# A hybrid SSD and attention trunk: the second projection issued between the first heads, and the diagonal products of a head pair taken in turn

## The chip, the cores and the metric

The kernel runs on one core of one Trainium2 chip. The metric is device time in microseconds, the median of several executions. A core has five engines that run at the same time, each with its own queue: TensorE (PE in the profile, with PEld for the loading of its stationary operand), VectorE (DVE), ScalarE (ACT), GpSimd (POOL) and SyncE (SP), which here only issues DMA transfers. Matrix products land in PSUM, which has eight banks here used as four "pa", three "pm" and one "po".

## The reference, cut to what matters

One sequence of 512 tokens with 1024 channels goes through two layers. The first layer mixes an RG-LRU and a Mamba-2 SSD, the second is softmax attention with 16 heads; each is followed by a SwiGLU FFN with 2816 hidden channels. Everything is float32. The change touches two places.

In the SSD, with 16 heads of 64 channels and chunks of 128 tokens, the part within a chunk is

```
y_diag = jnp.einsum('bclsgr,bcsgrp->bclgrp', cb[..., None] * decay, xdt)
```

that is, for each head and each of the four chunks, a 128 by 128 matrix (scores times decay) times the 128 by 64 inputs of that head.

In the attention layer the normed input is multiplied by one matrix that gives q, k and v of all heads; q and k are normed per head and partly rotated, then come scores, softmax and the product with v:

```
qkv = (h @ w_qkv).reshape(b, l, 3, ATT_HEADS, ATT_HEAD_DIM)
q = partial_rope(rmsnorm(qkv[:, :, 0], q_norm), pos) * (ATT_HEAD_DIM ** -0.5)
k = partial_rope(rmsnorm(qkv[:, :, 1], k_norm), pos)
```

The three dilated windows are merged into one softmax whose mask holds the logarithm of how many windows hold a key.

## The kernel before, in words

**Products.** Every large product is made of three fp32r products (low times high, high times low, high times high; `mm3`, L103 to L108, and L726 to L728 for q, k and v). For this each operand is split in two: `split` (L82 to L84) copies with rounding on ACT and subtracts on VectorE, or on GpSimd for the weights of the attention layer (`on_pool`, L80). `weight(i)` (L89) loads weight tile i and two ahead over SP's queue, 512 KB each, and splits them; raw, high and low tiles have three buffers each.

**SSD.** Two heads form a pair. `ssd_pair(j)` (L519) loads the cumulated decays of both heads, makes the decay matrices (L527 to L533) and leaves `ssd_out(j)` (L537) to be issued behind the next projection. `ssd_out` has the diagonal products, eight matmuls into one bank: head e of the pair writes partitions 64e to 64e+63, chunk c writes columns 128c to 128c+127, and its stationary operand has the 64 columns of that head (L543). Each of these fp32 matmuls shows up in the profile as two instructions. Then come three products with the carried states (L547) and three VectorE operations (L548 to L550). Pairs 0 to 3 run beside the RG-LRU, whose end (`lru_end`, L552) is a long chain on ACT and VectorE; pairs 4 to 7 run beside the gate projections.

**Attention.** The 16 heads are worked on in two halves of eight. `qkv_part(half, w)` (L711) gives four steps for w = 0, 1, 2 (q, k, v). A step takes one weight tile and issues 24 matmuls of 512 columns; four token tiles accumulate in the four "pa" banks over the four steps. The fourth step calls `finish_qk` (L737) for each of four token tiles: two ACT operations, a reduction, a power on GpSimd (L747), the scaling L748, and six small VectorE operations for the rotation (L752 to L757). For v it calls `finish_v` (L780), which writes the tiles v0 to v3; these have one buffer, so those of the second half are written when the first half has read its own.

`attend(half, between)` (L869) goes through eight heads:

```
            for h in range(first, first + 8):
                if h % 2 == 0 and h < first + 6:
                    pair_T(h // 2 + 1)
                if h < first + 7:
                    scores(h + 1)
                values(h)
                for st in between.get(h, ()):
                    st()
```

`pair_T` (L760) transposes q and k of a pair and splits them; `scores` (L796) makes the scores of a head (L808, L809) and its softmax on VectorE (L814, L816), ACT (L815) and GpSimd (L817); `values` (L821) transposes the probabilities (L835), splits them, and multiplies with v (L842, L843). Behind the first half stands the whole projection of the second half, 12 steps; the second half has parts of the output projection between its heads.

**What sets the order.** The program is unrolled. The framework that builds it arranges the instructions of each engine by itself ahead of time: the order in which they are written is their rank, and where a piece of higher rank is reckoned to wait for something, a piece of lower rank that is ready is put in. Buffers and data are guarded by semaphores. So the written order is a wish, and the order on TensorE can be read from the trace only.

Of the kernel before, what the change touches and what calls it, by code (L numbers as in the profile page):

```python
# [19 lines left out]
NT = T // P  # L20
# [38 lines left out]
def trunk(ctx: ExitStack, tc: tile.TileContext, a):  # L59
# [29 lines left out]
    def weight(i):  # L89
        while emitted[0] <= min(i + AHEAD, len(specs) - 1):  # L90
            j = emitted[0]
            src, n = specs[j]
            raw = wp.tile([P, WMAX], F32, tag="raw", bufs=NRAW, name=f"wr{j}")
            hi = wp.tile([P, WMAX], F32R, tag="whi", bufs=NSPL, name=f"wh{j}")
            lo = wp.tile([P, WMAX], F32R, tag="wlo", bufs=NSPL, name=f"wl{j}")
            step = n if j else n // 4
            for c in range(0, n, step):
                nc.sync.dma_start(out=raw[:, c:c + step], in_=src[:, c:c + step])
                split(raw[:, c:c + step], hi[:, c:c + step], lo[:, c:c + step], G if src.tensor.name in on_pool else V)
            w_of[j] = (hi, lo)  # L100
            emitted[0] += 1
        return w_of.pop(i, None)
# [54 lines left out]
    def pc(name, i=0, n=1):  # L157
        o, _ = _PV[name]
        return pv[:, o + i:o + i + n]
# [88 lines left out]
    with ExitStack() as rctx:  # L248
# [288 lines left out]
        def ssd_out(j, E, MT):  # L537
            g, jj = j // 4, j % 4
            pd = pm.tile([P, T], F32, tag="pm", name="ps_yd")
            for e in range(2):  # L540
                for c in range(NT):
                    s = slice(c * P, (c + 1) * P)
                    mm(pd[64 * e:64 * e + 64, s], lhsT=xdt[j][:, c, 64 * e:64 * e + 64], rhs=MT[e][:, s], start=True, stop=True)  # L543
            po = pm.tile([P, T], F32, tag="pm", name="ps_yo")
            for c in range(1, NT):
                s = slice(c * P, (c + 1) * P)
                mm(po[:, s], lhsT=prev[g, c - 1][:, jj * P:(jj + 1) * P], rhs=CT[g][:, s], start=True, stop=True)  # L547
            V.tensor_tensor(out=E[:, P:], in0=E[:, P:], in1=po[:, P:], op=ALU.mult)  # L548
            V.scalar_tensor_tensor(out=xs[j], in0=xs[j], scalar=pc("ssd_d", j), in1=pd, op0=ALU.mult, op1=ALU.add)
            V.tensor_tensor(out=xs[j][:, P:], in0=xs[j][:, P:], in1=E[:, P:], op=ALU.add)  # L550
# [128 lines left out]
    with ExitStack() as actx:  # L679
# [31 lines left out]
        def qkv_part(half, w):  # L711

            pss = []

            def step(kp):
                if kp == 0:
                    for t in range(NT):
                        pss.append(pa.tile([P, T], F32, tag="pa", name="ps_qkv"))
                wh, wl = weight(i_qkv[half, w, kp])
                for t in range(NT):  # L720
                    ts_ = slice(t * P, (t + 1) * P)
                    for k2 in range(2):
                        k = 2 * kp + k2
                        xh, xl = norm.hl[k]
                        cols = slice(k2 * T, (k2 + 1) * T)
                        mm(pss[t], lhsT=xl[:, ts_], rhs=wh[:, cols], start=(k == 0), stop=False)  # L726
                        mm(pss[t], lhsT=xh[:, ts_], rhs=wl[:, cols], start=False, stop=False)  # L727
                        mm(pss[t], lhsT=xh[:, ts_], rhs=wh[:, cols], start=False, stop=(k == KD - 1))  # L728
                if kp == 3:
                    for t in range(NT):  # L730
                        (finish_v if w == 2 else finish_qk)(half, w, t, pss[t])

            return [lambda kp=kp: step(kp) for kp in range(4)]
# [26 lines left out]
        def pair_T(pair):  # L760
            half, p = pair // 4, pair % 4
            for w in range(2):
                ps = pm.tile([P, T], F32, tag="pm", name="ps_qT")
                for t in range(NT):
                    nc.tensor.transpose(ps[:, t * P:(t + 1) * P], qk[half, w, t].rearrange("p h e -> p (h e)")[:, p * P:(p + 1) * P], ident)
                g = gains[w]

                hs_ = [ap_.tile([P, T], F32R, tag=f"hi{w}{e}", bufs=2, name="qk_hi") for e in range(2)]
                klo = None if w == 0 else kz[pair % 2]
                for e in range(2):  # L770
                    own = slice(64 * e, 64 * e + 64)
                    other = slice(64 - 64 * e, 128 - 64 * e)
                    S.activation(hs_[e][own], ps[own], AF.Copy, scale=g[own])  # L773
                    lo = hs_[e][other] if w == 0 else klo[e][own]
                    V.scalar_tensor_tensor(out=lo, in0=ps[own], scalar=g[own], in1=hs_[e][own].bitcast(F32), op0=ALU.mult, op1=ALU.subtract)
                    if w == 1:
                        S.activation(hs_[e][other], ps[own], AF.Copy, scale=g[own])
                qkT[pair, w] = hs_ if w == 0 else (hs_, klo)
# [73 lines left out]
        def out_proj(half, mp, after=None):  # L852
            w = weight(i_ao[half, mp])
            for m2 in range(2):
                ps = pa.tile([P, T], F32, tag="pa", name="ps_ao")
                for k in range(4):
                    c = (m2 * 4 + k) * P
                    mm3(ps, w, oT[4 * half + k], (slice(None), slice(c, c + P)), (slice(None), slice(None)), k == 0, k == 3)
                m = 2 * mp + m2
                V.tensor_tensor(out=x[m], in0=ps, in1=x[m], op=ALU.add)  # L860
                if after is not None:
                    after(m)
# [6 lines left out]
        def attend(half, between):  # L869
            first = 8 * half  # L870
            pair_T(first // 2)
            scores(first)
# [6 lines that stand above are left out]
                for st in between.get(h, ()):  # L879
                    st()  # L880

        attend(0, {})
        for w in range(3):
            for st in qkv_part(1, w):
                st()
        attend(1, {9: [lambda: out_proj(0, 0)], 12: [lambda: out_proj(0, 1)], 15: [lambda: out_proj(0, 2), lambda: out_proj(0, 3)]})
        for mp in range(4):
            out_proj(1, mp, norm3.feed)
# [94 lines left out]
```

## Time and profile before

| | before |
|---|---|
| median of 3 runs | 1359.38 us (1357.98 to 1360.65) |
| profiled execution | 1356.76 us, its span 1355.0 us |
| TensorE busy | 1329.4 us (98%) |
| VectorE / ScalarE / GpSimd busy | 794.5 / 573.2 / 151.3 us |
| mean granted TensorE clock | 0.998 |

Times in the rows count from the first instruction. The duration of a matmul in the profile is its way through the engine, and matmuls overlap: a 512-column product of the fp32r kind has a duration of 0.39 us while the next one starts 0.23 us after it. An engine is shown as idle only where no instruction is on its way. L-numbers are lines of the listing above; names such as ps_yd, ps_qkv, ps_s, ps_pT and ps_o are the PSUM tiles of the diagonal products, the projection, the scores, the transposed probabilities and the outputs.

### The profile page before, as it was taken

Reading aid. Unit: us, or ns where it says so; the run is one execution under the profiler, and the core shown is the slowest. Engines: PE = TensorE matmul, PEld = TensorE weight load, DVE = VectorE, ACT = ScalarE, POOL = GpSimd, SP = SyncE. Lnnn points to the kernel's source line nnn. Section 1 sums busy time; section 2 is a strip of 40 time slices with the busy share of each in tenths; the row PEclk is TensorE's granted clock in tenths of the full one; section 3 lists DMA queues with packets and bytes.
Section 4 is the critical chain, followed back from the end, with each engine's and each line's share of the span. In section 5 each row is a group of like instructions: output and inputs, shape, how many; then the busy total and the mean of one; then the engine's idle time right before and its main releaser. Section 6 shows DMA issues by size and latency. Waiting matters only on the chain.

```text
span 1355.0 us, 15685 instructions
## 1 busy us (share of the span) xinstructions
PE 1329.4 (98%) x6058; PEld 1074.7 (79%) x6058; DVE 794.5 (59%) x1332; ACT 573.2 (42%) x842; POOL 151.3 (11%) x127
## 2 busy tenths in 40 slices
PE   8999989999999999999999999999999999999998
PEld 6877767888888888888888877777788888888886
DVE  7887799865444434434453778788764434444442
ACT  6743867433333222312233479658643212222221
POOL 0000000000000000000005755554200000000000
PEclk9999999999999999999999999999999999999999
DMA  6322222532233333332232221221133333333232
GB/s 238 110 92 80 94 78 77 172 94 94 93 94 93 94 93 100 92 105 93 88 100 94 80 76 48 63 78 47 32 109 93 93 95 99 97 86 107 93 100 72
DMA packets 38554, 126.50 MB, mean 93 GB/s; under 512 B 4288, under 2 KB 5056, under 8 KB 38352
## 3 DMA queue, kind: packets, MB, share of 16 engines
q1 hardware_dynamic: 38480, 125.51, 29.7%
q8 instruction: 47, 0.77, 0.2%
q14 instruction: 27, 0.22, 0.1%
HBM read 123.36 MB, written 2.13 MB: 93 GB/s over the span
## 4 chain that ended last, share of the span: by engine, by line
PE 83%; DVE 8%; ACT 6%; POOL 1%; issue 1%; DMA 0%; SPq 0%; POOLq 0%; DVEq 0%; ACTq 0%
PE ps_pr L106 24%; PE ps_pr L107 24%; PE ps_pr L108 24%; ACT s L815 1%; PE ps_qkv L726 1%; PE ps_qkv L728 1%; PE ps_qkv L727 1%; POOL qrs L747 1%; DVE q L748 1%; ACT qk_hi L773 1%; PE ps_pT L835 1%; PE ps_yd L543 1%; PE ps_o L842 1%; ACT ph L83 1%; DVE q L756 1%
## 5 line engine op out<-in xcount | busy, mean ns | idle before, releaser
L83 ACT CAST wh<-wr 128x1024 fp32r<-128x1024 f32 (+2 forms) x223 | 228.1, 1024 | 629.8 <-PE ps_pr L108 396.1
L106 PE MATMUL ps_pr<-xh,wl 128*128 128x512 f32 x1056 | 415.9, 394 | 11.9 <-DVE wl L84 11.2
L107 PE MATMUL ps_pr<-xl,wh 128*128 128x512 f32 x1056 | 414.3, 392 | 0.9 <-DVE xl L183 0.9
L108 PE MATMUL ps_pr<-xh,wh 128*128 128x512 f32 x1056 | 412.8, 391 | 0.0
L84 DVE TENSOR_TENSOR wl<-wr,wh 128x1024 fp32r<-128x1024 f32 (+2 forms) x191 | 225.9, 1183 | 52.1 <-ACT wh L83 51.6
L106 PEld LDWEIGHTS ps_pr<-xh,wl 128*128 128x128 f32 x1056 | 199.2, 189 | 55.1 <-DVE wl L84 12.1
L107 PEld LDWEIGHTS ps_pr<-xl,wh 128*128 128x128 f32 x1056 | 199.2, 189 | 43.9 <-DVE xl L183 2.3
L108 PEld LDWEIGHTS ps_pr<-xh,wh 128*128 128x128 f32 x1056 | 199.1, 189 | 42.0 <-issue 0.7
L108 PE MATMUL ps_pr<-ah,wh 128*128 128x512 f32 x352 | 138.7, 394 | 0.0
L106 PE MATMUL ps_pr<-ah,wl 128*128 128x512 f32 x352 | 138.7, 394 | 0.0
L107 PE MATMUL ps_pr<-al,wh 128*128 128x512 f32 x352 | 138.7, 394 | 0.0
L84 POOL TENSOR_TENSOR wl<-wr,wh 128x1024 fp32r<-128x1024 f32 x32 | 79.1, 2475 | 395.7 <-ACT wh L83 392.6
L669 DVE TENSOR_TENSOR x<-ps_pr,x 128x512 f32<-128x512 f32 x48 | 33.2, 692 | 127.6 <-PE ps_pr L108 127.6
L661 DVE TENSOR_TENSOR tu<-ps_pr,nrb 128x512 f32<-128x512 f32 x44 | 30.4, 692 | 130.7 <-PE ps_pr L108 130.7
L659 DVE TENSOR_TENSOR tg<-ps_pr,nrb 128x512 f32<-128x512 f32 x44 | 30.4, 692 | 93.9 <-PE ps_pr L108 93.9
L107 PEld LDWEIGHTS ps_pr<-al,wh 128*128 128x128 f32 x352 | 65.8, 187 | 16.3
L108 PEld LDWEIGHTS ps_pr<-ah,wh 128*128 128x128 f32 x352 | 65.8, 187 | 16.3
L106 PEld LDWEIGHTS ps_pr<-ah,wl 128*128 128x128 f32 x352 | 65.8, 187 | 16.2
L726 PE MATMUL ps_qkv<-wh,xl 128*128 128x512 f32 x192 | 75.6, 394 | 0.6 <-ACT q L740 0.6
L728 PE MATMUL ps_qkv<-wh,xh 128*128 128x512 f32 x192 | 75.5, 393 | 0.0
L727 PE MATMUL ps_qkv<-wl,xh 128*128 128x512 f32 x192 | 75.5, 393 | 0.0
L726 PEld LDWEIGHTS ps_qkv<-wh,xl 128*128 128x128 f32 x192 | 36.1, 188 | 7.9 <-ACT q L740 1.0
(232 smaller groups left out, 1580.5 us busy)
## 6 DMA issues: line engine op xcount, KB each, us to landing
wr<-in_w_gu SPq DMA_DIRECT2D x88, 512.0 KB, 3.5
wr<-in_w_in SPq DMA_DIRECT2D x35, 512.0 KB, 3.5
wr<-in_w_dn SPq DMA_DIRECT2D x32, 448.0 KB, 3.4
wr<-in_w_qkv SPq DMA_DIRECT2D x24, 512.0 KB, 3.5
wr<-in_w_out SPq DMA_DIRECT2D x16, 512.0 KB, 3.5
wr<-in_w_dn SPq DMA_DIRECT2D x16, 512.0 KB, 3.5
x<-in_xT SPq DMA_DIRECT2D x16, 256.0 KB, 3.2
bcs<-csd SPq DMA_DIRECT2D x16, 256.0 KB, 4.4
```

The lines of the kernel that those rows point to most:

```text
L83: S.copy(hi, src)
L84: eng.tensor_tensor(out=lo, in0=src, in1=hi.bitcast(F32), op=ALU.subtract)
L106: mm(ps, lhsT=wl[ws], rhs=xh[xs], start=start, stop=False)
L107: mm(ps, lhsT=wh[ws], rhs=xl[xs], start=False, stop=False)
L108: mm(ps, lhsT=wh[ws], rhs=xh[xs], start=False, stop=stop)
L543: mm(pd[64 * e:64 * e + 64, s], lhsT=xdt[j][:, c, 64 * e:64 * e + 64], rhs=MT[e][:, s], start=True, stop=True)
L659: V.tensor_tensor(out=tg, in0=pg, in1=rb, op=ALU.mult)
L661: V.tensor_tensor(out=tu, in0=pu, in1=rb, op=ALU.mult)
L669: V.tensor_tensor(out=x[m], in0=ps, in1=x[m], op=ALU.add)
L726: mm(pss[t], lhsT=xl[:, ts_], rhs=wh[:, cols], start=(k == 0), stop=False)
L727: mm(pss[t], lhsT=xh[:, ts_], rhs=wl[:, cols], start=False, stop=False)
L728: mm(pss[t], lhsT=xh[:, ts_], rhs=wh[:, cols], start=False, stop=(k == KD - 1))
```

## The change

In `ssd_out` the two loops change places, so that the diagonal products of the two heads follow each other chunk by chunk. In the attention layer the 12 steps of the second half's projection are put into `attend(0, ...)`: two steps behind head 0, one behind head 1, and so on (2, 1, 2, 1, 2, 1, 2, 0), eleven in all; the last step, which holds `finish_v`, stands behind the first half as before. No operation is added or removed.

```
-            for e in range(2):
-                for c in range(NT):
+            for c in range(NT):
+                for e in range(2):
...
-        attend(0, {})
-        for w in range(3):
-            for st in qkv_part(1, w):
-                st()
+        steps = [st for w in range(3) for st in qkv_part(1, w)]
+        at_head, k = {}, 0
+        for h, n in enumerate((2, 1, 2, 1, 2, 1, 2, 0)):
+            at_head[h] = steps[k:k + n]
+            k += n
+        attend(0, at_head)
+        for st in steps[k:]:
+            st()
```

## Rows read from the trace of the kernel before

**Rows 1.** The page's first lines and its chain of waits, by engine and by line.

```profile
span 1355.0 us, 15685 instructions
PE 1329.4 (98%) x6058; PEld 1074.7 (79%) x6058; DVE 794.5 (59%) x1332; ACT 573.2 (42%) x842; POOL 151.3 (11%) x127
...
PE 83%; DVE 8%; ACT 6%; POOL 1%; issue 1%; DMA 0%; SPq 0%; POOLq 0%; DVEq 0%; ACTq 0%
```

**Rows 2.** The chain that ended last, in order of time, from 130 to 300 us: start, duration, what, and the count of instructions merged.

```profile
137.35 1.51 PE ps_yd L543 x16
...
157.64 0.87 ACT wh L83
...
192.94 1.51 PE ps_yd L543 x16
...
204.83 0.69 ACT ti L483
...
248.64 1.02 PE ps_yd L543 x8
...
262.74 1.51 PE ps_yd L543 x16
...
289.46 1.51 PE ps_yd L543 x16
```

**Rows 3.** Instructions of the tile ps_yd in three stretches of the block that starts at 262.67 us: stretch, its length, then busy time and count of each engine (an instruction counts in each stretch that it touches).

```profile
262.67:263.16 0.49, 0.49 (x4) 0.49 (x5) 0.00 (x0) 1.00 0.16 67
263.16:263.60 0.44, 0.44 (x10) 0.44 (x9) 0.00 (x0) 1.00 0.83 344
263.60:264.18 0.58, 0.58 (x8) 0.41 (x4) 0.00 (x0) 1.00 1.02 417
```

**Rows 4.** TensorE in order of time: start, duration, line, operation, tiles, count, and in brackets the idle time before it with what ended it. First a pair that is absent from rows 2, then the longest wait of the recurrent layer.

```profile
159.25 1.58 PE L543 MATMUL ps_yd<-bcs,xdt 128*64 128x128 f32 x16
...
182.20 0.79 PE L106 MATMUL ps_pr<-xh,wl 128*128 128x512 f32 x1 [4.16 <-DVE wl L84]
```

**Rows 5.** Busy time of every engine in the first half's heads, in the stretch behind them, and in the second half's heads: stretch, length, then PE, PEld, DVE, ACT, POOL with counts, granted clock, DMA share, GB/s.

```profile
791.00:866.00 75.00, 70.81 (x384) 55.19 (x383) 62.70 (x186) 63.78 (x139) 38.73 (x42) 1.00 0.17 50
866.00:899.00 33.00, 33.00 (x147) 27.28 (x146) 21.36 (x39) 14.19 (x19) 21.40 (x10) 1.00 0.26 81
899.00:972.00 73.00, 69.70 (x378) 54.10 (x377) 57.64 (x160) 57.82 (x130) 28.78 (x37) 1.00 0.13 44
```

**Rows 6.** The same two first stretches for the instructions of the tile ps_qkv alone (PE, PEld, DVE, ACT).

```profile
791.00:866.00 75.00, 40.19 (x144) 25.07 (x143) 2.58 (x4) 3.46 (x5) 1.00 0.17 50
866.00:899.00 33.00, 33.00 (x147) 27.28 (x146) 0.36 (x1) 4.81 (x7) 1.00 0.26 81
```

**Rows 7.** TensorE's two largest waits from 791 to 899.5 us: who waited for whom, total us, times, longest us.

```profile
PE ps_pT L835 <- DVE m L814: 2.7, 3, 2.3
PE ps_s L808 <- DVE kz L775: 0.4, 1, 0.4
```

**Rows 8.** TensorE in order of time: the one place where a projection waits for its bank, then two short waits among the heads and the longest.

```profile
773.61 0.50 PE L726 MATMUL ps_qkv<-wh,xl 128*128 128x512 f32 x1 [0.55 <-ACT q L740]
...
811.95 0.63 PE L835 MATMUL ps_pT<-cst,s 128*128 128x128 f32 x4 [0.19 <-DVE m L814]
...
819.65 0.39 PE L728 MATMUL ps_qkv<-wh,xh 128*128 128x512 f32 x1
820.22 0.30 PE L808 MATMUL ps_s<-kz,qk_hi 128*128 128x128 f32 x1 [0.18 <-DVE qk_hi L775]
...
856.06 0.40 PE L728 MATMUL ps_qkv<-wh,xh 128*128 128x512 f32 x1
858.77 0.87 PE L835 MATMUL ps_pT<-cst,s 128*128 128x128 f32 x6 [2.31 <-DVE m L814]
```

**Rows 9.** GpSimd in order of time from 846 us on, then VectorE in the stretch of the longest wait.

```profile
846.69 2.39 POOL L84 TENSOR_TENSOR wl<-wr,wh 128x1024 fp32r<-128x1024 f32 x1 [0.88 <-ACT wh L83]
849.07 0.69 POOL L817 TENSOR_SCALAR s<-s,m 128x512 f32<-128x512 f32 x1
...
853.51 2.40 POOL L84 TENSOR_TENSOR wl<-wr,wh 128x1024 fp32r<-128x1024 f32 x1
...
853.78 2.21 DVE L756 TENSOR_TENSOR q<-rtmp 128x64 f32<-128x64 f32 x1
855.91 0.21 DVE L757 TENSOR_TENSOR q<-rtmp 128x64 f32<-128x64 f32 x1
```

**Rows 10.** VectorE in order of time behind the first half's heads: its instructions above 2 us. Then the page of line L748: shortest, median and longest duration in ns.

```profile
868.60 2.48 DVE L84 TENSOR_TENSOR xl<-o,xh 128x512 fp32r<-128x512 f32 x1 [1.46 <-ACT xh L83]
...
881.67 2.88 DVE L748 TENSOR_TENSOR q<-q,qrs 128x512 f32<-128x512 f32 x1 [1.53 <-POOL qrs L747]
...
890.22 2.87 DVE L748 TENSOR_TENSOR q<-q,qrs 128x512 f32<-128x512 f32 x1 [1.25 <-POOL qrs L747]
...
893.02 2.42 DVE L756 TENSOR_TENSOR q<-rtmp 128x64 f32<-128x64 f32 x1
895.50 2.42 DVE L752 TENSOR_TENSOR rtmp<-q,rope1c 128x64 f32<-128x64 f32 x1
...
L748 DVE TENSOR_TENSOR q<-q,qrs x16: 674/693/2877, 747.3 to 890.2; 128x512 f32<-128x512 f32 x16
```

**Rows 11.** The page's DMA issues of the projection's weights: count, KB each, us from issue to landing.

```profile
wr<-in_w_qkv SPq DMA_DIRECT2D x24, 512.0 KB, 3.5
```

## The prediction, as it was put on record

> **What bounds the kernel now.** The page's first lines and its chain come first: TensorE is busy for 1329.4 of 1355.0 us, and 83% of the chain is its own work [rows 1]. So a part of the change is worth what it takes off TensorE's queue, or off TensorE's waits, in a stretch where nothing else ends last; that has to be read stage by stage. No instruction is added or taken away, so only overlap and waits can change. For the SSD I read the chain in order of time [rows 2], since it tells which blocks of diagonal products lie on the path, and the instructions of ps_yd by stretches [rows 3]. For the attention layer I read the busy time of all engines in three stretches [rows 5]: in the heads of the first half TensorE is idle for 75.00 - 70.81 = 4.2 us with VectorE at 84% and ScalarE at 85%, and in the 33 us behind them it is never idle. Then its waits [rows 7, 8], and what the engines before it were doing [rows 9, 10].
>
> The rows on ps_qkv are the surprise: the projection of the second half, written behind the first half's heads, is not run there alone. Of its 288 matmuls some 138 (144 in the stretch, less 6 that end the first half's own v) lie among the heads, and the rest behind [rows 6]. The framework fills the waits with it already: 138 / 24 = 5.8 of 12 steps, where the new text asks for 11.
>
> **Part 1: the diagonal products in turn.** A block has 16 instructions, eight for each head of the pair. Where only one head's eight stand together they take 1.02 us on the chain (248.64); where all sixteen stand together they take 1.51 us, and not twice as much [rows 2]. The stretches tell why: for the first 0.49 us four instructions of ps_yd are touched, then ten in 0.44 us [rows 3], so the second head's instructions, which write the other 64 partitions, run beside the first head's last ones. Written in turn, both heads should run side by side from the start, and a block should take what one head takes: 1.51 - 1.02 = 0.49 us less. Bounds: 0 if the overlap needs the long run of one head; 0.49; below nothing, if taking turns kept the two heads apart altogether, a block would take two runs of eight, 2.04 us, 0.53 more than now, 2.7 us in the five blocks that count. I take 0.49, the nearest row: in the stretch of ten both heads are at work together.
>
> Which blocks count: the three from 262.74 to 289.46 lie on the chain with TensorE work on both sides, 3 x 0.49 = 1.47. Those at 137.35 and 192.94 lie on it too, ahead of the points where the chain goes over to ScalarE (157.64 and 204.83) [rows 2]: ScalarE starts earlier by as much, 0.98. The block at 159.25 comes after the chain has left TensorE, which then waits 4.16 us for the split of a weight tile that is late on VectorE [rows 4]; the 0.49 makes this wait longer and is worth nothing, and the same holds for the fourth pair, behind 204.83. The block at 248.64 stands there as eight because the second head's matrix was not reckoned to be ready; I count 0, as it will be late in any order. Sum: 2.45 us, between +2.7 and -3.4 (seven blocks).
>
> The Trainium skill speaks against this part: "TensorE: Matmul & The Clock Gate", section "Part 3: Packing small matmuls", says that matmuls start and end strictly in program order, and that a load of weights overlaps a running matmul only where the row group differs, which it does not here. By that rule the order of the two heads is worth 0, a rival below. The same section says that outputs on different partition groups of PSUM run at the same time, and by that the 2.45 stand. The trace agrees with the second: sixteen take 1.51 us and not 2 x 1.02.
>
> **Part 2: the moved projection.** TensorE's work is the same. What can go is the idle time among the heads, 4.2 us [rows 5]. Of it 2.31 is one wait at 858.77 and 0.45 the wait of the very first scores for kz (0.4 in rows 7), ahead of any moved step. The other 1.4 us is in twelve short pieces, like those at 811.95 and 820.22. Such a piece costs more than is shown: at 820.22 the next start comes 0.57 us after the last one, in place of 0.23, so 0.34 is lost where 0.18 is shown as idle [rows 8]. The 0.16 on top belongs to each. Two pieces (0.25) fall into heads 0 and 1, at 811.95 and before it, where the order can hardly change. The ten left are 1.2 + 10 x 0.16 = 2.8 us. A step now outranks the next heads, so TensorE has 24 matmuls of 0.23 us between a head's scores and its values, and softmax gets the time: I take all 2.8 off. Bounds: 0, and 5.8 (all idle but the first scores, 3.74, and 13 x 0.16).
>
> What the move adds. Besides the 24 matmuls, each step issues one 512 KB transfer, 3.5 us to landing [rows 11], one ScalarE cast and one GpSimd subtraction. On SP nothing else stands in these stretches but later weights in the same order, so the transfers cost nothing. On GpSimd a split takes 2.39 us and a head's normalisation stands behind it (846.69, 849.07) [rows 9]; today six splits lie among the heads, tomorrow about eleven. TensorE's next matmuls cover that, as they do in this case. The fourth step of a group brings four finishes with it. The q group's four lie among the heads already, the k group's four move there from the 33 us in which TensorE waits for nothing and VectorE is at 65% [rows 5]. The wait of 2.31 us shows the price: at 853.78 VectorE's L756 takes 2.21 us (its like, L757, takes 0.21 right behind) while GpSimd splits a weight tile (853.51 to 855.91); behind it in VectorE's queue stand the next tiles' steps and the reciprocals and maxima of softmax, for which ScalarE and then TensorE wait [rows 8, 9]. Behind the heads five such instructions stand [rows 10]. One of them per group is the nearest count (one stall of 2.31 + 0.16 = 2.5 us from the q group's finishes); half of it I take as covered by the steps that now rank ahead: +1.2. Bounds: 0 and 5 x 2.5 = 12.4.
>
> The last step brings finish_v behind the first half's last values, and the output projection needs its four banks. A projection that waited for a bank lost 0.55 us [rows 8]; I take that, +0.55. Bounds: 0, and the 2.31 of the longest wait.
>
> Sum of part 2: -2.8 + 1.2 + 0.55 = -1.05.
>
> **Sum.** -2.45 - 1.05 = -3.5 us. Against its own time, the profiled execution's 1356.76 (span 1355.0 and 1.76 around), that is 1353.3. That execution lies 2.6 below the median of the runs, so on the median of 1359.38 it is 1355.9. A measurement of this kernel tells some 0.2% (2.7 us) from no change: the forecast is on the edge of what can be seen.
>
> **Rivals.**
>
> Everything goes well (16%): all waits among the heads that can go do, 5.8, with no new stall, and seven blocks give 3.4: 9.2 less, 1350.2. For it: TensorE's work sets these stretches and ScalarE and VectorE have 16% to spare. Against: the order is fixed ahead and does not know of L756 at 2.21 us.
>
> Slower, by the k finishes (18%): four of the five long VectorE instructions of rows 10 now stop softmax in the midst of the heads and TensorE each time by 2.5 us, 9.9 in all; less 2.45, 2.8 and plus 0.55 that is +5.2, 1364.6. At two stalls it is a draw, from the third on it is slower. For it: 881.67, 890.22, 893.02 and 895.50 are all of the k group, L748 at 2.88 where its median is 0.69. Against: they stand close to each other behind a string of splits at full speed of the projection, and splits will come more slowly between heads. The Trainium skill, "SBUF — State Buffer", section "Who interferes with whom", has the rule behind it: a VectorE instruction with two SBUF inputs and a GpSimd instruction that reads SBUF exclude each other for their whole length. By it each of the moved finishes can meet a split, and the time would be that of this rival; the trace agrees at 853.78.
>
> The order of the heads is worth nothing on TensorE (15%): part 2 alone, 1358.3. For it: only long runs show the overlap. Against: 1.51 against 1.02 us.
>
> The move changes nothing (11%): the framework has filled the waits already, and goes on filling with what is ready; gain and loss of part 2 cancel, part 1 alone, 1356.9.
>
> **How the numbers follow.** The forecast has 40%, its own range 1353.9 to 1357.9 (one term of part 2 or two blocks more or less). Faster by over 0.2% (below 1356.7): three quarters of the forecast, 0.30, the first rival, 0.16, half of the last, 0.05, and 0.02 of the third: 0.53. Within 0.2%: 0.10 of the forecast, 0.12 of the third, 0.06 of the last, 0.01 of the second: 0.29. Slower: 0.17 of the second, 0.01 of the third: 0.18. The range of 8 in 10 leaves out half of the first rival and most of the second: 1351 to 1362.
>
> **What would show it.** In the profile after: the sixteen instructions of a block within 1.02 us, and five or more blocks that are shorter on the chain; the wait at 182.20 not shorter than 4.16 less 0.1. Among the first heads some 264 matmuls of ps_qkv and not 138, a stretch with less than 2.5 us of idle TensorE, and the pieces of 0.1 to 0.2 us fewer; the k group's L748 to L757 between softmax operations, with at most one above 2 us that TensorE waits behind. Wrong would be: blocks of 1.5 us; several waits of 2 us or more of ps_pT or ps_o; a wait of TensorE for finish_v; or the same 4 us of idle time at other places.

## The result and the profile after

The changed kernel takes 1372.24 us (median of 4 runs, 1371.53 to 1373.55) against 1359.43 us for the kernel before on the same chip: ratio 1.0096, 95% interval 1.0078 to 1.0113, so 13 us slower. The forecast was 1355.9 in a range of 1351 to 1362; the sign was wrong. The profiled execution took 1372.17 us. Its page, first lines and chain of waits, beside [rows 1]:

```profile
span 1370.1 us, 15687 instructions
...
PE 1331.2 (97%) x6058; PEld 1074.8 (78%) x6058; DVE 791.3 (58%) x1332; ACT 574.0 (42%) x842; POOL 150.3 (11%) x127
...
PE 83%; DVE 9%; ACT 5%; POOL 2%; issue 1%; DMA 0%; SPq 0%; POOLq 0%; DVEq 0%; ACTq 0%
```

The span grew by 15.1 us and TensorE's busy time by 1.8, so nearly all of it is idle time of TensorE, or 13.3 us. On the chain GpSimd goes from 1% to 2% and VectorE from 8% to 9%. First the SSD: the chain in order of time, as in [rows 2].

```profile
137.46 1.02 PE ps_yd L543 x16
...
193.10 1.02 PE ps_yd L543 x16
...
261.82 0.36 PE ps_yd L543 x2
262.19 0.42 PE ps_yo L547 x2
262.61 1.02 PE ps_yd L543 x14
...
275.29 1.02 PE ps_yd L543 x16
...
288.16 1.02 PE ps_yd L543 x16
```

Sixteen instructions now take 1.02 us where they took 1.51, as forecast, in four of the five blocks that were to count. The fifth (262.74 before) was taken apart by the framework: two of its instructions, then two of ps_yo, then the rest, 0.36 + 1.02 = 1.38 us for its own. The late weight split still ends the wait of 4.16 us in [rows 4]. TensorE goes on 0.37 us earlier than before, and the wait became longer by about what the block before it got shorter:

```profile
181.83 0.80 PE L106 MATMUL ps_pr<-xh,wl 128*128 128x512 f32 x1 [4.63 <-DVE wl L84]
```

The attention layer then starts 1.75 us earlier (first transpose of q at 789.68 and not 791.43), so everything that was lost was lost behind that. TensorE's waits from 789 to 1000 us, total, times and longest, against [rows 7], which end with the first half (of the 15.5 us, 14.6 fall there):

```profile
PE ps_pT L835 <- DVE m L814: 15.5, 7, 8.0
PE ps_s L808 <- DVE qk_hi L775: 1.8, 2, 1.7
```

Before, the transposes of the probabilities waited 2.7 us for softmax maxima in the first half's heads. Now two of these waits are 8.0 and 5.7 us long. The stretches around the first, with columns as in [rows 5], the one behind the second, and the second half's heads at the end:

```profile
829.00:837.80 8.80, 8.80 (x46) 7.51 (x44) 6.36 (x14) 4.57 (x8) 5.25 (x3) 1.00 0.16 49
837.80:846.20 8.40, 0.37 (x3) 0.04 (x1) 6.54 (x19) 1.41 (x3) 5.00 (x4) 0.73 0.24 73
846.20:851.90 5.70, 5.70 (x19) 4.74 (x20) 3.88 (x19) 3.73 (x10) 3.04 (x5) 0.50 0.00 1
...
882.14:886.00 3.86, 3.86 (x11) 3.20 (x12) 2.36 (x11) 1.35 (x3) 1.77 (x2) 0.50 0.08 33
...
915.00:988.00 73.00, 69.88 (x379) 54.14 (x378) 56.40 (x158) 57.82 (x130) 28.84 (x37) 1.00 0.12 37
```

For 8.4 us TensorE does next to nothing (0.37 us), ScalarE little (1.41), and even VectorE and GpSimd are not full (6.54 and 5.00 of 8.40): a chain that goes back and forth between engines. The second half's heads are as before (69.88 of 73.00 busy against 69.70). VectorE in order of time from 829 us on, with only the lines that carry the argument:

```profile
829.08 0.68 DVE L744 TENSOR_REDUCE qss<-qsq 128x8 f32<-128x512 f32 x1
...
831.73 0.69 DVE L748 TENSOR_TENSOR q<-q,qrs 128x512 f32<-128x512 f32 x1 [1.76 <-POOL qrs L747]
...
833.20 2.10 DVE L753 TENSOR_TENSOR rtmp<-q,rope0s 128x64 f32<-128x64 f32 x1
...
838.26 0.69 DVE L748 TENSOR_TENSOR q<-q,qrs 128x512 f32<-128x512 f32 x1 [0.71 <-POOL qrs L747]
...
840.87 2.82 DVE L748 TENSOR_TENSOR q<-q,qrs 128x512 f32<-128x512 f32 x1 [1.25 <-POOL qrs L747]
...
845.36 0.68 DVE L814 CUSTOM_DVE_ANT_0 s<-ps_s,cst 128x512 f32<-128x512 f32 x1
```

and GpSimd beside it:

```profile
830.05 1.65 POOL L747 TENSOR_TENSOR qrs<-qss,mhalf 128x8 f32<-128x8 f32 x1 [3.00 <-DVE qss L745]
832.82 2.39 POOL L84 TENSOR_TENSOR wl<-wr,wh 128x1024 fp32r<-128x1024 f32 x1 [1.13 <-ACT wh L83]
836.59 1.64 POOL L747 TENSOR_TENSOR qrs<-qss,mhalf 128x8 f32<-128x8 f32 x1 [1.37 <-DVE qss L745]
839.18 1.66 POOL L747 TENSOR_TENSOR qrs<-qss,mhalf 128x8 f32<-128x8 f32 x1 [0.95 <-DVE qss L745]
840.81 2.33 POOL L84 TENSOR_TENSOR wl<-wr,wh 128x1024 fp32r<-128x1024 f32 x1
```

This is the finish of the q group. The scores of the next head are ready at 837 us, but its first maximum (L814, 845.36) stands in VectorE's queue behind the q group's token tiles. From 829.08 to 845.36, 16.3 us, VectorE is on them (and on one short addition that ends a head), and only about half of that is work. It waits three times for the power on GpSimd, 1.76 + 0.71 + 1.25 = 3.7 us, and twice an instruction is held up while GpSimd splits a weight tile: L753 takes 2.10 us (its like take 0.22), L748 takes 2.82 (0.69), so 1.88 + 2.13 = 4.0 us. Without these 7.7 us the maximum could have come that much earlier, if nothing else had held the tiles, and that is most of TensorE's wait of 8.03 us. This is a reckoning; the runs below test it. TensorE in order of time:

```profile
837.77 0.40 PE L728 MATMUL ps_qkv<-wh,xh 128*128 128x512 f32 x1
846.19 1.09 PE L835 MATMUL ps_pT<-cst,s 128*128 128x128 f32 x4 [8.03 <-DVE m L814]
...
847.93 0.63 PE L728 MATMUL ps_qkv<-wh,xh 128*128 128x512 f32 x1
848.36 0.63 PE L726 MATMUL ps_qkv<-wh,xl 128*128 128x512 f32 x1
```

After the wait the next matmuls start 0.43 us apart and not 0.23: the granted clock of that stretch is 0.50, the 1.2 GHz level, and it had been 1.00, the 2.4 GHz level, until TensorE stopped. Seven matmuls of 512 columns took from 846.93 to 850.07, 3.1 us in place of 1.6, so the stall cost at least 1.5 us more than it shows, and the stretch at 0.50 lasts until 851.90.

The k group's finish does the same a second time: L748 waits 1.82 and 1.53 us, and lasts 2.82 in the second case, 2.13 too long; together 5.5 us, against 5.71 us of the wait that follows.

```profile
873.61 0.69 DVE L748 TENSOR_TENSOR q<-q,qrs 128x512 f32<-128x512 f32 x1 [1.82 <-POOL qrs L747]
...
877.36 2.82 DVE L748 TENSOR_TENSOR q<-q,qrs 128x512 f32<-128x512 f32 x1 [1.53 <-POOL qrs L747]
...
881.31 0.68 DVE L814 CUSTOM_DVE_ANT_0 s<-ps_s,cst 128x512 f32<-128x512 f32 x1
```

```profile
882.14 1.09 PE L835 MATMUL ps_pT<-cst,s 128*128 128x128 f32 x4 [5.71 <-DVE m L814]
```

The clock is at 0.50 behind this wait too, from 882.14 to 886.00. With that the loss adds up. From the first transpose of q of the first half to that of the second, before and after:

```profile
791.43:899.47 108.04, 103.85 (x530) 82.50 (x529) 84.10 (x226) 77.98 (x157) 60.13 (x52) 1.00 0.19 59
```

```profile
789.68:914.87 125.19, 107.77 (x530) 85.98 (x528) 81.09 (x227) 78.87 (x157) 59.06 (x52) 0.93 0.16 55
```

The stretch grew by 17.2 us for the same 530 instructions of TensorE: its idle time from 4.2 to 17.4 us, 13.2 more, and its busy time by 3.9 us, for which the 9.6 us at clock 0.50 have room (half of them, 4.8, at most).

Each engine's order is fixed when the program is built, so it can be read without a clock. VectorE's queue in the first half's heads, one letter per instruction: S a softmax maximum (L814), p the split of transposed probabilities, o the addition that ends a head, Q a scaling L748 (one per token tile's finish), V a v finish. Both strings begin with the first head's splits.

```
before  pppSoSSSpppoSSSSpppSoSSSpppSoSSSQpppQSoSSSpppSQSoSSpppQpoppoQQQQVVVV
after   pppoSSSSpppoSSSSpppQoQQSQSSSpppoSSSSpppoQQSQQSSSpppSoSSSpppopppVoVV
```

Before, the q group's four finishes stand singly among the later heads, and the k group's four behind all heads. After, three tiles of the q group (with one addition between) and two of the k group stand in one run ahead of the maxima of a head that is waited for, and the next tile's reduction with them.

### The profile page after: what moved, and what is told of

Read it like the earlier page. It is cut to its first block, busy times and chain, and to the rows that moved or that the text cites. A ratio compares the mean times of both kernels' runs of the same rounds, so it can differ in the third digit from the quotient of the medians.

```text
span 1370.1 us, 15687 instructions
## 1 busy us (share of the span) xinstructions
PE 1331.2 (97%) x6058; PEld 1074.8 (78%) x6058; DVE 791.3 (58%) x1332; ACT 574.0 (42%) x842; POOL 150.3 (11%) x127
## 3 DMA queue, kind: packets, MB, share of 16 engines
HBM read 123.36 MB, written 2.13 MB: 92 GB/s over the span
## 4 chain that ended last, share of the span: by engine, by line
PE 83%; DVE 9%; ACT 5%; POOL 2%; issue 1%; DMA 0%; SPq 0%; POOLq 0%; DVEq 0%; ACTq 0%
PE ps_pr L106 24%; PE ps_pr L107 24%; PE ps_pr L108 24%; POOL qrs L747 2%; DVE q L748 1%; PE ps_qkv L728 1%; PE ps_qkv L727 1%; PE ps_qkv L726 1%; ACT s L815 1%; PE ps_pT L835 1%; PE ps_o L842 1%; PE ps_o L843 1%; DVE s L814 1%; PE ps_yd L543 1%; DVE qss L744 0%
## 5 line engine op out<-in xcount | busy, mean ns | idle before, releaser
L84 DVE TENSOR_TENSOR wl<-wr,wh 128x1024 fp32r<-128x1024 f32 (+2 forms) x191 | 225.8, 1183 | 52.1 <-ACT wh L83 51.6
L84 POOL TENSOR_TENSOR wl<-wr,wh 128x1024 fp32r<-128x1024 f32 x32 | 78.5, 2458 | 406.2 <-ACT wh L83 406.1
L107 PEld LDWEIGHTS ps_pr<-al,wh 128*128 128x128 f32 x352 | 65.8, 187 | 16.3
```

The costliest lines, as they stand in the source:

```text
L84: eng.tensor_tensor(out=lo, in0=src, in1=hi.bitcast(F32), op=ALU.subtract)
L107: mm(ps, lhsT=wh[ws], rhs=xl[xs], start=False, stop=False)
```

## The experiments

Theory: what was lost is VectorE's time on a lump of finishes that stands ahead of softmax, stretched by trips to GpSimd (power) and by GpSimd's splits. Rivals: the moved matmuls themselves, by outranking the heads' own work; the alternation; the mere place of the lump, whatever its length.

**Each part alone.** `alternate_only` is the kernel before with the first hunk of the change, `move_only` the changed kernel without it.

> Only the diagonal products alternate; the projection stands as before. The trace of the changed kernel has blocks of 0.82 us from first to last start in place of 1.31, and its first attention transpose comes 1.7 us earlier (789.7 against 791.4). If the alternation does what it seems to do, this kernel is 1.5 to 2.5 us faster than before and its attention layer is unchanged. If the alternation disturbs something else as well (a rival, since two blocks have been taken apart in the changed kernel), it is 0 to 2 us slower.

> Only the projection is moved; the diagonal products stand as before. The changed kernel is 12.8 us slower than before by its median and spends 17 us more between the first attention transpose and the last output projection of the first half's kind. If the whole loss comes from the move, this kernel is 14 to 17 us slower than before. If the two edits disturb each other, it is less than 12 us slower.

Measured: the alternation alone 1356.49 us, ratio 0.9978 (0.9970 to 0.9987); the move alone 1373.85, ratio 1.0106 (1.0093 to 1.0120). The alternation is worth 3.0 us of 1359.4; the move costs 14.4 alone and 15.7 on top of the alternation. The loss is the move's, wholly.

**The finish later, or the scores earlier.** Two attempts to put softmax ahead by the order of the text. `finish_late` writes the second half's squares, reductions, powers and rotations behind the first half's heads:

```
+            if half == 0:
+                rest()
+            else:
+                late.append(rest)
...
         attend(0, at_head)
+        for f in late:
+            f()
```

> The changed kernel, but of the q and k finishes only the copy that frees the bank stays behind the fourth step; square, reduction, power, scaling and rotation are written behind the first half's heads, so they rank last. If the rank of the finishes is the cause (they stand in VectorE's queue ahead of the next head's softmax because they are written ahead of it), the waits of 8.0 and 5.7 us go and the kernel is within 3 us of before. If the rank of the steps' matmuls is the cause (a step of 24 outranks the next head's scores, VectorE is reckoned idle for that time, and low-ranking finishes are put there just the same), two finishes still stand ahead of softmax and half of the loss or more stays: 5 to 12 us slower than before.

Measured: 1374.13, ratio 1.0107 (1.0093 to 1.0121), no gain. VectorE's queue still has finishes ahead of maxima, now two by two (`oQQSSSSpppQQoSSSS`). I take it that the framework reckons VectorE to be idle while a step's 24 matmuls run and puts in what is ready, whatever its rank; the run fits that and does not show it. Writing the finishes last did not take the lumps away. `scores_first` gives the next head's transposes, scores and maxima a rank 130 instructions earlier:

```
+                with tc.high_priority(offset=130) if half == 0 else ExitStack():
+                    if h % 2 == 0 and h < first + 6:
+                        pair_T(h // 2 + 1)
+                    if h < first + 7:
+                        scores(h + 1)
```

> The changed kernel, but in the first half the transposes and scores of the next head rank ahead of the step that stands between (an offset of 130 instructions), while steps and finishes stand where the change put them. If the steps' rank over the scores is the cause, softmax stands ahead of the finishes in VectorE's queue, TensorE has no wait above 3 us among the heads, and the kernel is between 4 us faster and 2 us slower than before. If the amount of finish work among the heads is the cause (VectorE's and GpSimd's time, wherever it stands), it is 6 us or more slower than before.

Measured: 1373.30, ratio 1.0100 (1.0085 to 1.0116). The maxima did move ahead of the finishes, and the wait only changed its name: TensorE's largest waits are now for the split of the probabilities (L84), with the lump ahead of it.

```profile
PE ps_qT L765 <- DVE pl L84: 10.7, 2, 10.4
PE ps_s L808 <- DVE pl L84: 3.4, 1, 3.4
```

**Early finishes without moved matmuls.** The text of before, its projection written behind the heads, but the second half's q and k finishes ranked 430 instructions earlier:

```
+                        if half == 1 and w < 2:
+                            with tc.high_priority(offset=RAISE):
+                                finish_qk(half, w, t, pss[t])
...
+        RAISE = 430
```

> The kernel before, with the projection written behind the heads so that its matmuls fill waits as before, but with the second half's q and k finishes ranked 430 instructions earlier, about where the change puts them. The diagonal products stand as before. If a lump of finishes ahead of softmax costs the time by itself, TensorE gets waits of several us here too and the kernel is 4 us or more slower than before. If it takes the steps' matmuls in one run as well (because TensorE then has nothing left to fill a wait with), it is within 3 us of before.

Measured: 1369.58, ratio 1.0079 (1.0064 to 1.0094), 10.3 us slower than before. The longest wait:

```profile
PE ps_s L813 <- DVE qk_hi L780: 9.7, 3, 9.4
```

(this kernel's L813 and L780 are L808 and L775 of the others). Only the q group's finishes came among the heads by this, the k group's stayed behind them. Finishes in a lump ahead of attention work cost 9.4 us in one place with no matmul given a higher rank.

**What makes the lump long.** `no_power` replaces the GpSimd power by a copy on VectorE, `split_on_vector` leaves the power and makes the splits of the projection's weights on VectorE; the rest is the changed kernel.

```
-            G.tensor_tensor(out=rs, in0=ss, in1=mhalf[:, :8], op=ALU.pow)
+            if half == 0:
+                G.tensor_tensor(out=rs, in0=ss, in1=mhalf[:, :8], op=ALU.pow)
+            else:
+                V.tensor_copy(rs, ss)
```

```
-    on_pool = ("in_w_qkv", "in_w_ao")
+    on_pool = ("in_w_ao",)
```

> The changed kernel with the power on GpSimd left out of the second half's q and k finishes: VectorE copies the mean squares in its place, so the norm of these q and k is not applied. In the two runs before, a lump of four finishes stood in VectorE's queue between pieces of softmax wherever it was written, and VectorE waited for a power of 1.65 us four times in it. If these round trips to GpSimd make the lump too long, TensorE's two long waits (8.0 and 5.7 us) shrink to less than 3 us each and the kernel is 7 to 13 us faster than the changed one, at 1359 to 1365. If the splits on GpSimd, which shut VectorE out, make it too long, the waits shrink by no more than 2 us each and it is at 1368 or more.

> The changed kernel with the splits of the projection's weights on VectorE and not on GpSimd, so that GpSimd never shuts VectorE out of a finish and powers and normalisations stand behind no split. VectorE gets 24 subtractions of 1.2 us more. If the exclusion is the cause (long instructions of 2.1, 2.8 and 2.8 us in the two lumps, and powers behind splits), it is 4 to 10 us faster than the changed kernel. If the power's round trips are the cause, it is within 3 us of it, or slower because VectorE has more to do.

Measured: 1360.96 without the power, ratio 1.0013 (1.0004 to 1.0023), 11.3 us off; 1364.75 with the splits on VectorE, ratio 1.0044 (1.0028 to 1.0061), 7.5 us off. What is left in the first is the other cause: its longest wait is 4.7 us, and VectorE in that stretch shows two instructions at more than ten times their usual 0.2 us, both while GpSimd splits:

```profile
832.62 2.40 DVE L759 TENSOR_TENSOR q<-rtmp 128x64 f32<-128x64 f32 x1
...
838.88 2.31 DVE L745 TENSOR_SCALAR qss<-qss 128x8 f32<-128x8 f32 x1
```

(2.40 - 0.21) + (2.31 - 0.16) = 4.3 of 4.7 us. So the wait did not fall below the 3 us that I expected, though the time came out in the range given. `no_power_split_vector` has both edits.

> The changed kernel with both things removed that stretch a lump of finishes: the power of the second half's q and k is replaced by a VectorE copy (so their norm is not applied) and the splits of the projection's weights run on VectorE. Alone the first took off 11.3 us and the second 7.5, from 15.7 (1372.2 less the 1356.5 of the alternation alone). If the two parts of the lump overlap (the power waits behind a split on GpSimd, and VectorE is shut out by a split, at the same time), the sum is below 18.8 and the time is that of the alternation alone, 1356 to 1359. If a lump costs by its mere place ahead of softmax, a part stays: 1361, as without the power alone.

Measured: 1353.04, ratio 0.9960 (0.9945 to 0.9975). Together they take off 19.2 us, against 11.3 + 7.5 = 18.8 for each alone, so no overlap of the two is to be seen, and it is more than the loss of 15.7. The longest wait of ps_pT for a maximum is 0.5 us, although finishes still stand ahead of maxima in VectorE's queue (`oQQSQSQSS`): their mere place, with none of them stretched, costs little. No run has both edits without the move, so how much of the 3.5 us below the alternation alone is due to the norm left out isn't shown; the same comparison with nothing left out follows below. This kernel skips the norm, so it is no candidate.

**One power for four tiles.** `one_power` collects the four tiles' sums in one 128x32 tile and takes one power per group; results are as before.

```
+            ss = at.tile([P, NT * 8], F32, tag="qss4", name="qss4", bufs=1)
...
+            G.tensor_tensor(out=ss, in0=ss, in1=mhalf[:, :NT * 8], op=ALU.pow)
```

> The changed kernel with one power per group for all four token tiles of the second half (32 columns) in place of four powers in a row (8 columns each); results are unchanged. If the round trips are the cause, this takes three of four away and the kernel is 4 to 10 us faster than the changed one. If the exclusion by splits is the cause, it is within 3 us of it.

Measured: 1370.18, ratio 1.0084 (1.0069 to 1.0099), 2 us off only. GpSimd's power and VectorE behind it:

```profile
837.00 5.44 POOL L775 TENSOR_TENSOR qss<-qss,mhalf 128x32 f32<-128x32 f32 x1 [0.45 <-DVE qss L774]
```

```profile
842.47 3.42 DVE L780 TENSOR_TENSOR q<-q,qss 128x512 f32<-128x512 f32 x2 [5.55 <-POOL qss L775]
```

The power goes by its columns: 5.44 us for 32, against 4 x 1.65 = 6.6 for four times 8. One trip of this kind is nearly as long as four, and VectorE waits for it in one piece of 5.55 us. So this edit did not shorten the lump much, and the run doesn't tell the trips from the splits, although a result within 3 us is what I had put down for the splits.

**Fewer steps moved.** Only the tuple of steps behind each head differs: (2, 1, 0, 0, 0, 0, 0, 0) and (2, 1, 2, 1, 1, 0, 0, 0).

> The changed kernel with only the first three of the 12 steps between the heads (two behind head 0, one behind head 1), so that no fourth step, and with it no finish of q or k, is moved; nine stay behind the heads as before. If the loss comes from the four finishes that a fourth step puts in a lump into VectorE's queue, nothing of it is left: 1356.5 us, as with the alternation alone, and no wait of ps_pT above 2.5 us. If the moved matmuls themselves cost, by ranking ahead of the attention work of the next heads, 3 of 11 steps keep their part of the 16 us: about 1361.

> The same kernel as three_steps (1362.5 us, 6 above the alternation alone, though no finish was moved by its text), for a profile that can be laid beside the others. If finishes of the q group meet the heads here too, singly and at other places than before, the waits are several of 1 to 3 us for a softmax maximum or a transposed q behind a finish. If the moved matmuls themselves cost, TensorE's waits are no longer than with the alternation alone (4.2 us among the first heads) and the heads end later for another reason.

> The changed kernel with the first seven steps between the heads (2, 1, 2, 1, 1), so that the q group's four finishes are moved and the k group's are not. If each lump has its own price, the first wait of 8 us near 838 stays with the slow matmuls behind it, and the one of 5.7 near 876 goes: about 10 us above the alternation alone, 1366 to 1367. If the framework puts the k group's finishes among the heads in any case, as it did with a part of them before, both stay: 1372.

Measured: three steps ratio 1.0027 (1.0015 to 1.0039) and, measured again, 1362.24 us, ratio 1.0028 (1.0016 to 1.0040); seven steps 1364.79, ratio 1.0047 (1.0034 to 1.0061). Seven go as the price per lump says, if a little under the 1366 to 1367 given: the first wait stays, the second is gone, and the time lies between.

```profile
PE ps_pT L835 <- DVE m L814: 10.8, 7, 8.0
```

Three steps are a miss. I expected nothing to be left, and some 5.7 us against the alternation alone are. TensorE's waits among the first heads up to 870 us, and VectorE ahead of the longest:

```profile
PE ps_pT L835 <- DVE m L814: 3.8, 3, 1.6
PE ps_s L808 <- DVE qk_hi L775: 3.7, 1, 3.7
```

```profile
839.83 2.87 DVE L748 TENSOR_TENSOR q<-q,qrs 128x512 f32<-128x512 f32 x1 [1.18 <-POOL qrs L747]
```

With the alternation alone the same stretch has 2.7 for the maxima and at most 0.2 for anything else but the 0.4 of the first scores that both have. The fourth step is not moved by the text here, but the framework fills it in earlier than before, and the q group's finishes meet the heads singly; one of them, held 2.87 us by a split that started at 839.76, delays the transposed q of the next pair. So it doesn't take a lump: one finish in the wrong place costs what stretches it. The added waits are some 4.6 of the 5.7 us. Behind the wait of 3.7 us the granted clock is at the lower level again:

```profile
848.30:851.70 3.40, 3.40 (x14) 2.82 (x14) 3.37 (x12) 3.19 (x10) 3.40 (x3) 0.53 0.04 10
```

Between the two halves' first transposes TensorE's busy time is 104.91 us against 103.82 with the alternation alone; this 1.1 us, for which the 3.4 us at 0.53 have room, is the rest.

**Both stretchers removed with nothing left out.** The power of the second half is made on ScalarE as exp(-ln(x)/2), once per group in the way of `one_power`, and the splits run on VectorE; with the move (`ln_group_split`) and without it (`alt_ln_group_split`). Two more tell the parts apart without the move: `alt_ln_group` (splits left on GpSimd) and `alt_split_vector` (power left on GpSimd).

```
+            S.activation(ss, ss, AF.Ln)
+            S.activation(ss, ss, AF.Exp, scale=-0.5)
```

> The changed kernel with both stretchers of the lump taken away and nothing left out: the power of q and k of the second half is made on ScalarE as exp(-ln(x)/2), once for the four tiles of a group (two ScalarE table loads of 1.28 us each per group), and the splits of the projection's weights run on VectorE. If the loss is the length of the lump, most of the 15.7 us goes: 1355 to 1359. If a lump costs by its place whatever its length, 1361 or more.

> The alternation alone with both: power on ScalarE per group and splits of the projection's weights on VectorE. If both causes of waits are gone, 1353 us, as the moved kernel without the power; if VectorE with 24 splits more sets the pace of the first heads, 1357 as with the splits on VectorE alone.

> The alternation alone with the second half's power made on ScalarE in the same way, the splits left on GpSimd. If the waits that the alternation alone still has among the first heads (a 2.3 us one of them) come from the trip to GpSimd, 1354 us; if from the splits, 1356.5; if the four reductions that now stand together ahead of the first rotation stop softmax, 1358 or more.

> A candidate for the best: the kernel before with the alternation, the projection as written before, and the splits of the projection's weights on VectorE. If the 2.31 us wait of the kernel before, which stood behind a VectorE instruction held up by a split on GpSimd, is such a case and VectorE has room for 24 splits more of some 1.2 us each, 1354 us, 2.5 below the alternation alone. If VectorE sets the pace of the first half's heads (84% busy there), the splits cost as much or more there: 1357 to 1360.

Measured, ratios to before with their intervals:

| power, splits | alternation alone | alternation and move |
|---|---|---|
| GpSimd, GpSimd | 0.9978 (0.9970 to 0.9987) | 1.0096 (1.0078 to 1.0113) |
| GpSimd, VectorE | 0.9989 (0.9980 to 0.9998) | 1.0044 (1.0028 to 1.0061) |
| ScalarE, GpSimd | 0.9994 (0.9985 to 1.0003) | not tried |
| ScalarE, VectorE | 0.9982 (0.9974 to 0.9991) | 0.9987 (0.9978 to 0.9996) |

In the last row the move costs 0.0005, or 0.7 us, less than can be told from nothing: 1357.31 against 1356.55 us. In the first it costs 0.0118, or 16 us. So the rival of the moved matmuls falls: with the finishes short they cost nothing that shows. TensorE's largest waits in the attention layer of the moved kernel, and the page of its scaling line (shortest, median, longest in ns):

```profile
PE ps_o L875 <- DVE pl L84: 4.9, 5, 2.0
...
PE ps_pT L868 <- DVE m L847: 1.3, 6, 0.4
...
L781 DVE TENSOR_TENSOR q<-q,qss x8: 679/684/693, 841.0 to 877.5; 128x512 f32<-128x512 f32 x8
```

No scaling is held up any more, and the waits for maxima fall from 15.5 to 1.3 us. The finishes stand elsewhere, though, behind a head's maxima and ahead of its splits (`oSSSSQQQQppp`), and the largest waits are now for those splits (L84), 4.9 us in five. The trip to ScalarE is not free either: a table load of 1.28 us stands ahead of the logarithm (L775) and another ahead of the softmax exponential (L848) that comes next:

```profile
837.48 1.28 ACT L775 ACT_TABLE_LOAD   x1
838.78 0.23 ACT L775 ACTIVATE qss<-qss 128x32 f32<-128x32 f32 x1
839.03 1.28 ACT L848 ACT_TABLE_LOAD   x1
840.72 0.21 ACT L776 ACTIVATE qss<-qss 128x32 f32<-128x32 f32 x1
```

Without the move neither edit gains: 0.9989, 0.9994 and 0.9982 against 0.9978. My hopes of 1353 and 1354 us were misses; the few waits of the kernel before are not worth these edits. No complete version is faster than the alternation alone, 1356.49 us.

## Why the prediction was wrong

**Part 1 was right.** Sixteen instructions in 1.02 us, a wait for the late split no shorter than before, and 3.0 us (1.8 to 4.1) by `alternate_only` against 2.45 in the sum. One of the five blocks gained 0.13 and not 0.49 us, since the framework took it apart. The rival that the order of the heads is worth nothing fell by the same run and by the 1.02 us. With it fell what the prediction drew from the Trainium skill's "TensorE: Matmul & The Clock Gate", section "Part 3: Packing small matmuls", that by strict order of starts and ends the order is worth 0. Whether starts and ends keep the program's order is not tested by that.

**Part 2 failed in one term: "+1.2" for the finishes.** It took one held-up instruction per group, 2.5 us, and covered half of it. On the chip the k and q groups cost waits of 5.7 and 8.0 us and, by the granted clock of 0.50 behind them, some 3.9 us more. Three things were wrong in that step. It priced one instruction where the finishes of several tiles come as one run in an in-order queue; all that stretches any of them adds up until the maximum gets through, two held instructions and up to three waits for the power in one lump. It counted only held instructions, 4.0 of the 7.7 us in the q group's run, and left out the trip to GpSimd for the power, 3.7, though [rows 10] shows such a wait in brackets beside each long L748 (1.53 and 1.25). And the q group was taken as known, since "four lie among the heads already": they lay there singly, and the new order put three of them in one run ahead of a head's maxima. The upper bound, 5 x 2.5 = 12.4 us, was near the truth (14 to 16), and I gave it too little weight.

**The "-2.8" for short waits** assumed that "softmax gets the time" of the 24 matmuls. The order on VectorE gave time to the finishes instead: besides the two long waits TensorE is idle among the heads for 17.4 - 13.7 = 3.7 us, where before it was 4.2 - 2.3 = 1.9 besides the one. That the move brings nothing even where the lumps are short is shown by the last row of the table (0.9982 without the move, 0.9987 with it): there the rival "the move changes nothing" holds.

**The "+0.55" for finish_v** did not show: the list of TensorE's waits from 789 to 1000 us, down to 0.3 us, has none for it. No run tested it alone.

**The second rival** had the right sign and half of the mechanism. Its lock is the one that the Trainium skill describes in "SBUF — State Buffer", section "Who interferes with whom", and the trace agrees: each of the VectorE instructions above 2 us that are shown here stands beside a split, and with the splits on VectorE (`split_on_vector`) none of L748 is above 0.70 us. Its price, four instructions of 2.5 us, left out the power and the run, and so came out at 1364.6 in place of 1372.2. Taking the splits away returned 7.5 us, which is this rival's part, and taking the power away 11.3, the part that no rival had.

**A reading that was off.** Of the 144 matmuls of ps_qkv counted among the heads [rows 6] three and not six belong to the first half's v, by their starts up to 791.20 us; the count is 141, or 5.9 steps, and no term of the sum hangs on it.

**Of the signs named beforehand** the blocks of 1.02 us came true; the ones that were to prove it wrong came true as well, several waits of 2 us or more of ps_pT. Some 264 projection matmuls among the first heads were asked for; they did get there, only the heads got longer with them:

```profile
789.68:876.00 86.32, 54.67 (x199) 36.95 (x199) 2.11 (x4) 5.74 (x9) 0.94 0.17 55
876.00:915.00 39.00, 24.57 (x91) 17.26 (x89) 2.08 (x3) 2.27 (x4) 0.91 0.16 55
```

Up to 915 us, where the second half's heads begin, the second half's 288 matmuls of ps_qkv (of the 290 one is counted twice and one is the first half's) are spread over the whole stretch, in place of 147 that ran by themselves at its end [rows 6].

## What to carry to other kernels

Before moving work forward to fill a wait, follow not its big instructions but its tail: whatever its last step sets off on other engines (here four tiles of reduce, power, scale, rotate) enters in-order queues, and the critical work behind it waits for the whole run with all of its trips to other engines. Price such a run by its length on the chip, idle time and held instructions included, as read where it already stands alone; here the order that the framework made ahead of time did not allow for it. Count the slower clock behind a stall of TensorE as well, as it stood behind the waits of 8.0, 5.7 and 3.7 us here. If it must move, first make the run short: no slow trip to another engine in its midst, and nothing beside it that can lock its engine out.

## What the runs showed of the hardware that was not expected

GpSimd's power costs by the column: 1.65 us for 128x8 and 5.44 for 128x32, so (5.44 - 1.65) / 24 = 0.16 us for each further column, and one power in place of four saves only 6.6 - 5.4 = 1.2 us. An instruction with a single tensor input can be held by a split as well: L745, a multiply-add of 128x8, took 2.31 us in place of 0.16 while GpSimd split from 838.43 to 841.16 us. In the alternating block at 137.39 us the instructions start in pairs 7 ns apart (0, 7, 160, 167 ns, by the single records of the trace), where the written order has the two heads in turn, and all sixteen take the 1.02 us of one head's eight [rows 2]. So the two halves of the output partitions run side by side from the first matmul on.
